# One weight split, the banks of some transposes, the squares of a recurrence and two pads in an encoder layer

## The chip, the cores and the metric

The kernel runs on one core of a Trainium2 chip. The metric is the device time of one execution in microseconds (us). The kernel before has a median of 1216.63 us over three runs, from 1215.02 to 1218.22.

A core has five instruction queues that run side by side and meet only at semaphores: TensorE (PE, matrix products into PSUM; PEld are its weight loads), VectorE (DVE), ScalarE (ACT), GpSimd (POOL) and SyncE (SP, which issues the DMAs here). Within a queue the order is fixed when the program is built. PSUM has eight banks of 128 x 512 fp32 values; TensorE writes them, VectorE and ScalarE empty them.

## The reference

One layer of an encoder over 1024 tokens of width 1024, all in fp32:

```python
h = x + hybrid_mixer(rms_norm(x))          # 8 heads of attention beside a gated linear recurrence
h = h + conv_glu_ffn(rms_norm(h))
return rms_norm(h)

# in hybrid_mixer, for both directions:
a = exp(-8 * sigmoid(xc @ w_a + b_a) * softplus(-lam))
u = sqrt(1 - a * a) * sigmoid(xc @ w_x + b_x) * xc
h_t = a_t * h_(t-1) + u_t                  # forward and reverse; the two are added
y_lru = gelu(lru_g) * h_sum                # then rms_norm over its 512 channels

# conv_glu_ffn:
u = depthwise_conv(xn @ w_up)              # 1024 -> 2 * 2816, three taps along the tokens
return (silu(u[:2816]) * u[2816:]) @ w_down
```

## The kernel before

Every fp32 operand of a product is split into two rounded parts, "hi" and "lo", and three products (hi hi, hi lo, lo hi) are summed. ScalarE mostly writes hi, VectorE or GpSimd lo = source - hi (`split`, lines 59 to 67). A product over 512 contracted values is so 12 matmuls of 128 x 512.

The recurrence works on four channel tiles j = 0 to 3. For each tile TensorE computes the projections into psx and psG and four gates into psg; ScalarE makes tanh, exp and square of them, VectorE and GpSimd scale, scan in two directions and merge into `y_lru`. `squares` (line 239) adds y_lru squared into `qs`: ScalarE squares into a scratch tile, GpSimd adds. The sum is read only at attention step 48. In the loop over j = 0 and 1 the order on TensorE is as written, that of the other engines is set by a scheduler when the program is built; from tile 2 on all are as written.

The FFN's up product uses a seven-product scheme: for each of 22 tiles of hidden channels `prod(1)` to `prod(7)` (line 1060, `PRODUCTS`) multiply sums of token halves (B11, B21, B22, T1 to T4) by sums of weights (W[0] to W[3]). Results lie in eight named PSUM banks: S, T, VL[0], VH[0], VL[1], VH[1], GL, GH.

The seam is the stretch between the output mix and the FFN loop. There the last token tiles are normalised and the eight forms are built: `tr_sum` transposes 128 x 512 values into a spare bank (four instructions of TensorE, line 941), ScalarE and VectorE split them into B[f] ("evict" below). `spare()` hands out banks in turn from the list `spares`. Products of the tiles 0 and 1 are written between the transposes. The weights come by DMA into three staging buffers (pool stp); a fetch is issued when all readers of the buffer's former content are done. The order is as written, but a scheduler may move instructions at the place where the ordered section ends and the next begins (before the FFN loop).

SBUF tiles come from pools on the left and on the right; a right-hand pool grows downward from the top, so a tile that is taken first shifts all tiles of later right-hand pools. Of the operands that TensorE reads T1, T3, T4, cT, wo345, kt1, xch, wn and yl lie on the right; T2, B11, B21, B22, kt0 and all FFN weights lie on the left. In the built program the right-hand ones named begin 32 bytes past a multiple of 64, the left-hand ones on a multiple of 64.

Of the kernel before, what the change touches and what calls it, by code (L numbers as in the profile page):

```python
# [10 lines left out]
F32 = mybir.dt.float32  # L11
# [6 lines left out]
P = 128  # L18
D = 1024
S = 1024  # L20
NT = S // P
# [9 lines left out]
CH = 2  # L31
NCHUNK = NPAIR // CH
EPS = 1e-6
GK = math.sqrt(2.0 / math.pi)

V_CW, V_CB, V_GB, V_LAM, V_GO, V_FW, V_FB = 0, 16, 20, 36, 44, 52, 184
# [4 lines left out]
def encoder_layer(ctx, tc, x, w_in, wq, wk, wv, gw, wo, wup, wdn, vec, g_mix, g_ffn, g_fin, g_q, g_kv, tab_t, tab_n, out):  # L41
    nc = tc.nc
    act, dve, pool, pe = nc.scalar, nc.vector, nc.gpsimd, nc.tensor
# [4 lines left out]
    def sbpool(name, bufs=1, side="left"):  # L48
        return tc.tile_pool(name=name, bufs=bufs, side=side, reuse_waits="tile")
# [10 lines left out]
    def split(hi, lo, src, hi_on="act", lo_on="dve"):  # L60
        if hi_on == "act":
            act.activation(hi, src, AF.Copy)  # L62
        elif hi_on == "dve":
            dve.tensor_copy(hi, src)
        else:
            pool.tensor_scalar(out=hi, in0=src, scalar1=1.0, scalar2=1.0, op0=ALU.mult, op1=ALU.mult)
        (dve if lo_on == "dve" else pool).tensor_tensor(out=lo, in0=src, in1=hi.bitcast(F32), op=ALU.subtract)  # L67
# [68 lines left out]

    right = ExitStack()
    keep = right.enter_context(sbpool("keep", side="right"))
    ctp = ExitStack()
    ctpool = ctp.enter_context(sbpool("ctpool", side="right"))  # L140
    cT = ctpool.tile([P, 2, 3, S], F32R, tag="cT", name="cT")
# [73 lines left out]
    def root():  # L215
        act.activation(bc[:, 0:2, :], bc[:, 0:2, :], AF.Sqrt, scale=-0.0625)
# [22 lines left out]
    def squares(j, t1, eng="act"):  # L239
        if j == 0:  # L240
            act.activation(qs, y_lru[:, j, :], AF.Square)
            return
        if eng == "act":
            act.activation(t1, y_lru[:, j, :], AF.Square)
        else:
            pool.tensor_tensor(out=t1, in0=y_lru[:, j, :], in1=y_lru[:, j, :], op=ALU.mult)
        pool.tensor_tensor(out=qs, in0=qs, in1=t1, op=ALU.add)
# [4 lines left out]
    if True:  # L252
        with sbpool("xp", side="right") as xp:
# [37 lines left out]
                xT.append([xtp.tile([P, NK, 512], F32R, tag="xT", name=f"xT{hf}{z}") for z in range(2)])  # L291
            lat = keep.tile([P, NT, NAT], F32, tag="keepB", name="lat")
            kp_nat = keep.tile([P, S], F32R, tag="kpT", name="kpT")
            ss_x = xp.tile([P, NT], F32, name="ss_x")
            ss_l = xp.tile([P, NT, 2], F32, name="ss_l")

            def square(i):
# [162 lines left out]
        if True:  # L460
            def conv_a(j):
                p = psx[j]
                xc = lp.tile([P, S], F32, tag=f"xc{j % 2}", name=f"xc{j}")
                cw = lambda t: vv[:, V_CW + 4 * j + t:V_CW + 4 * j + t + 1]
                act.activation(xc, p, AF.Identity, scale=cw(2), bias=vv[:, V_CB + j:V_CB + j + 1])
                dve.scalar_tensor_tensor(out=xc[:, 2:], in0=p[:, :-2], scalar=cw(0), in1=xc[:, 2:], op0=ALU.mult, op1=ALU.add)
                dve.scalar_tensor_tensor(out=xc[:, 1:], in0=p[:, :-1], scalar=cw(1), in1=xc[:, 1:], op0=ALU.mult, op1=ALU.add)
                dve.scalar_tensor_tensor(out=xc[:, :-1], in0=p[:, 1:], scalar=cw(3), in1=xc[:, :-1], op0=ALU.mult, op1=ALU.add)
                return xc

            def conv_b(j, xc):
                xch = lp.tile([P, 2, S], F32R, tag="xch", name=f"xch{j}")
                split(xch[:, 0], xch[:, 1], xc, "dve", "dve")
                return xc, xch

            def conv(j):
                return conv_b(j, conv_a(j))

            def gate(j, d, g):
                gwt, xch = got[f"g{j}"], cv[j][1]  # L480
                psg = bigA(f"psg{j}{d}{g}")
                b = 2 * d + g
                for hf in range(2):
                    mm3(psg[:, ts(hf, 512)], (gwt[:, 0, b, :], gwt[:, 1, b, :]),
                        (xch[:, 0, ts(hf, 512)], xch[:, 1, ts(hf, 512)]), True, True)
                act.activation(bc[:, 2 * g + d, :], psg, AF.Tanh, scale=0.5, bias=gb_h[:, 4 * j + b:4 * j + b + 1])

            def gated(j, d):
                dve.scalar_tensor_tensor(out=bc[:, 2 + d, :], in0=bc[:, 2 + d, :], scalar=1.0, in1=cv[j][0], op0=ALU.add, op1=ALU.mult)

            def a_tiles(j):
                return [lp2.tile([P, S], F32, tag="a", bufs=2, name=f"a{j}{d}") for d in range(2)]

            def a2_tile(j, d):
                return lp.tile([P, S], F32, tag="a2", name=f"a2{j}{d}")

            def t1_tile(j):
                return (lp2 if j % 2 else lp).tile([P, S], F32, tag="gt", name=f"t1{j}")

            def load_gates(j, gst=None):  # L500
                if gst is None:
                    gst = stp.tile([P, 4, P], F32, tag="st", name=f"gst{j}")
                    nc.sync.dma_start(out=gst, in_=gw[:, j])
                g = lp.tile([P, 2, 4, P], F32R, tag="gw", name=f"gwt{j}")
                split(g[:, 0], g[:, 1], gst, "act", "pool")
                return g

            got = {"X1": wx1, "G0": wG0, "g0": load_gates(0, gst0)}

            def load(k, j):  # L510
                got[f"{k}{j}"] = load_gates(j) if k == "g" else load_w((0 if k == "X" else 512) + j * P, f"w{k}{j}", w_in, "act")

            cv = {0: conv(0)}
            proj_x(1, got["X1"])
            cv[1] = conv(1)
            order.close()
            order.enter_context(tc.manual_schedule(engines=ORDER_PE))
            for j in range(2):
                load("X", j + 2)
                aa = a_tiles(j)  # L520
                gate(j, 0, 0)
                gate(j, 1, 0)
                for d in range(2):
                    a2 = a2_tile(j, d)
                    decay_exp(j, d, aa[d])
                    square_a(aa[d], a2)
                    decay_tanh(j, d)
                    decay_mul(d, a2)
                proj_g(j, got[f"G{j}"], 0)
                gate(j, 0, 1)  # L530
                gate(j, 1, 1)
                root()
                for d in range(2):
                    gated(j, d)
                    scale_in(d)
                    scan(d, aa[d])
                add_dirs(dve)
                proj_g(j, got[f"G{j}"], 1)
                t1 = t1_tile(j)
                gelu_a(t1, psG[j])  # L540
                gelu_b(t1, psG[j])
                load("g", j + 1)
                load("G", j + 1)
                proj_x(j + 2, got[f"X{j + 2}"])
                if j == 0:
                    cv[2] = conv(2)
                merge(j, t1, dve)
                squares(j, t1)
            load("G", 3)


# [21 lines left out]
    proj_g(2, got["G2"], 1)  # L573
    decay_mul(1, a2)
    root()
    gated(2, 0)
    gated(2, 1)
    scale_in(0)
# [3 lines left out]
    t1 = t1_tile(2)  # L582
# [315 lines left out]
    hh, B, raw = [], {}, {}  # L898
    with sbpool("op", side="right") as op:
# [62 lines left out]
        def tr_sum(f, j, one):  # L962
            src = {"T1": hh[j][:, 0:512], "T2": hh[j + 4][:, 512:1024], "T3": hh[j + 4][:, 0:512], "T4": hh[j][:, 512:1024]}[f]
            to_form(f, j, src, one)
# [54 lines left out]
        W = {(z, 0): wo345[:, z].rearrange("p z (k n) -> p z k n", k=NK) for z in range(1)}  # L1019
# [35 lines left out]
        S1, T1 = bank("S", "s1"), bank("T", "t0")  # L1055
        VL, VH = [None, None], [None, None]
        for j in range(2):
            VL[j], VH[j] = bank(f"L{j}", f"vl{j}"), bank(f"H{j}", f"vh{j}")
        GL, GH = bank("GL", "gl0"), bank("GH", "gh0")
# [10 lines left out]
    def prod(n, j, ps, new):  # L1070
        z, ko, f = PRODUCTS[n]
        w, b = W[z, j], B[f]
        for k in range(4):
            for l, r, a_, z_ in ((0, 0, new and k == 0, False), (0, 1, False, False), (1, 0, False, k == 3)):
                pe.matmul(ps, w[:, l, ko + k, :], b[:, r, k, :], start=a_, stop=z_, skip_group_check=True)  # L1075
# [7 lines left out]
    W[0, 1] = wo345[:, 1].rearrange("p z (k n) -> p z k n", k=NK)  # L1083
    c0 = stp.tile([P, S], F32, tag="st", name="c0")
    tr_sum("T2", 0, spare)
    prod(1, 0, VL[0], True)
    sums_a(7, dve)
    tr_sum("T2", 1, spare)
    tr_sum("T2", 2, spare)
    split(W[0, 1][:, 0], W[0, 1][:, 1], raw[1][0], "act", "dve")  # L1090
    copy(c0[:, lo], VL[0])
    prod(2, 0, GL, True)
    tr2(7, spare)
# [11 lines left out]
    fp = fpx.enter_context(sbpool("fp", side="right"))  # L1105
    for f in ("T1", "T3", "T4"):
        B[f] = fp.tile([P, 2, 4, 512], F32R, name=f)
    C11 = {1: fp.tile([P, S], F32, tag="c", bufs=4, name="s1c")[:, lo]}
    for j in range(3):
        tr_sum("T1", j, spare)  # L1110
    copy(C11[1], S1)
    add(C11[1], VL[1], C11[1])
    prod(6, 0, VL[0], False)
    tr_sum("T1", 3, spare)
    for j in range(3):
        tr_sum("T3", j, spare)
    copy(c0[:, hi], VL[0])
    spares.remove(T1)
    prod(5, 0, T1, True)
    tr_sum("T3", 3, spare)  # L1120
    for j in range(4):
        tr_sum("T4", j, spare)
# [207 lines left out]
    for j in range(1, NPAIR):  # L1330
# [20 lines left out]
        if j == 1:  # L1351
            GH = bank("GH", f"gh{j}")
# [173 lines left out]
```

## Time and profile before

| | us |
|---|---|
| median of three runs (lowest, highest) | 1216.63 (1215.02, 1218.22) |
| the profiled execution, its own time | 1217.72 |
| span of its trace | 1215.9 |
| PE busy in the span | 1165.4 |
| DVE busy | 925.7 |
| ACT busy | 656.4 |
| POOL busy | 241.9 |

The profiled execution takes 1217.72 us, of which the trace spans 1215.9; 1.8 us lie around it. TensorE is busy in 96% of the span, so a look at the whole shows little: what counts are the few places where it waits, and what they wait for. In the page, digits are tenths of busy time in 40 equal slices of 30.4 us. In a timeline, a row gives start, duration, engine, line, operation and, in brackets, how long the engine sat idle before and what ended it. PEclk is the granted clock of TensorE, 1.00 at 2.4 GHz and 0.50 at 1.2 GHz.

### The profile page before, as it was taken

To read this page: it belongs to the slowest core of one execution; us is meant where nothing else is said; L and a number is where in the kernel's file an instruction comes from. 1 tells how busy PE (TensorE), PEld (TensorE's weight loads), DVE (VectorE), ACT (ScalarE), POOL (GpSimd) and SP (SyncE) were. 2 spreads that over 40 slices of the span, in tenths; PEclk is the share of its full clock that TensorE was granted. 3 is DMA by queue.
4 is the path that set the end of the run, shared out by engine and by line. 5 is a ranking of instruction groups with operands and counts; after the bars stand their busy time and mean duration, and the time that the engine had idled before them with its cause. 6 is when DMAs were issued, how large, how long until landed. Compare 5 with 4: busy or idle time off the path is not lost.

```text
span 1215.9 us, 15339 instructions
## 1 busy us (share of the span) xinstructions
PE 1165.4 (96%) x5668; PEld 970.0 (80%) x5668; DVE 925.7 (76%) x1371; ACT 656.4 (54%) x1055; POOL 241.9 (20%) x138
## 2 busy tenths in 40 slices
PE   5999997999999999998999999999999999999997
PEld 5977775788889888776778888888888888888885
DVE  6787879777777755587687877877787876887866
ACT  5736687776777763343554454444454454443453
POOL 2213435621212433352011110101011000000000
PEclk9999989999999999998999999999999999999999
DMA  5311101000000142230243223332323259753233
GB/s 214 98 42 44 44 18 35 18 1 1 1 1 1 53 157 87 73 118 18 61 130 122 96 78 111 106 113 81 110 95 121 87 173 334 262 183 112 96 113 121
DMA packets 93579, 113.38 MB, mean 93 GB/s; under 512 B 5184, under 2 KB 59840, under 8 KB 93504
## 3 DMA queue, kind: packets, MB, share of 16 engines
q1 hardware_dynamic: 93504, 112.40, 27.9%
q8 instruction: 44, 0.72, 0.3%
q14 instruction: 31, 0.25, 0.1%
HBM read 82.76 MB, written 28.57 MB: 92 GB/s over the span
## 4 chain that ended last, share of the span: by engine, by line
PE 82%; DVE 10%; ACT 3%; DMA 2%; issue 2%; SPq 0%; DVEq 0%; POOL 0%; ACTq 0%
PE vl L1075 19%; PE x L1268 9%; PE y L1268 7%; PE gh L1075 5%; PE gl L1075 4%; PE pt L762 4%; PE p L1075 4%; PE av L773 3%; PE av L772 3%; PE sc L70 2%; PE sc L71 2%; PE sc L72 2%; DVE bc L223 2%; PE pso L71 1%; PE pso L72 1%
## 5 line engine op out<-in xcount | busy, mean ns | idle before, releaser
L1075 PE MATMUL vl<-T,w 128*128 128x512 f32 x792 | 195.7, 396 | 1.8 <-ACT gl L1081 1.5
L1075 PEld LDWEIGHTS vl<-T,w 128*128 128x128 f32 x792 | 148.6, 188 | 37.6 <-ACT gl L1081 1.9
L67 POOL TENSOR_TENSOR w<-rg,w 128x1024 fp32r<-128x1024 f32 x21 | 52.0, 2474 | 363.6 <-ACT w L62 212.3
L62 ACT ACTIVATE ptb<-pt 128x512 fp32r<-128x512 f32 x128 | 70.1, 596 | 57.5 <-PE pt L762 56.3
L748 DVE TENSOR_REDUCE nm<-sc 128x1 f32<-128x1024 f32 x64 | 78.2, 1222 | 29.9 <-PE sc L72 29.6
L67 DVE TENSOR_TENSOR ptb<-pt,ptb 128x512 fp32r<-128x512 f32 x128 | 83.1, 681 | 7.0 <-ACT ptb L62 7.0
L755 ACT ACTIVATE pr<-sc,nm 128x1024 f32<-128x1024 f32 x64 | 71.7, 1121 | 4.2 <-DVE nm L748 4.1
L762 PE MATMUL pt<-ident,pr 128*128 128x128 f32 x512 | 67.7, 274 | 3.8 <-DVE ptb L67 3.8
L762 PEld LDWEIGHTS pt<-ident,pr 128*128 128x128 f32 x512 | 59.2, 140 | 14.7 <-DVE ptb L67 6.0
L1075 PE MATMUL gh<-B,w 128*128 128x512 f32 x264 | 64.4, 393 | 1.4 <-DVE T L67 1.4
L1172 ACT ACTIVATE c<-gh,vv 128x512 f32<-128x512 f32 x22 | 17.1, 778 | 89.1 <-DVE gh L1078 89.1
L772 PE MATMUL av<-ptb,vt 128*128 128x256 f32 x256 | 64.9, 292 | 0.0
L773 PE MATMUL av<-ptb,vt 128*128 128x256 f32 x256 | 62.6, 283 | 0.0
L1075 PE MATMUL p<-T,w 128*128 128x512 f32 x252 | 62.5, 397 | 0.0
L1268 PE MATMUL x<-abS 128*128 128x512 f32 x264 | 60.2, 389 | 0.0
L1268 PE MATMUL y<-abS 128*128 128x512 f32 x264 | 60.2, 389 | 0.0
L1075 PEld LDWEIGHTS gh<-B,w 128*128 128x128 f32 x264 | 49.5, 188 | 13.0 <-DVE T L67 1.6
L1075 PE MATMUL vl<-B,w 128*128 128x512 f32 x240 | 58.4, 392 | 0.0
L1268 PEld LDWEIGHTS x<-abS 128*128 128x128 f32 x264 | 49.6, 188 | 10.3
L1268 PEld LDWEIGHTS y<-abS 128*128 128x128 f32 x264 | 49.6, 188 | 10.3
L1075 PE MATMUL gl<-B,w 128*128 128x512 f32 x240 | 57.7, 389 | 0.0
L1075 PEld LDWEIGHTS p<-T,w 128*128 128x128 f32 x252 | 47.4, 188 | 11.4
(646 smaller groups left out, 2953.8 us busy)
## 6 DMA issues: line engine op xcount, KB each, us to landing
rg<-in_wup SPq DMA_DIRECT2D x22, 512.0 KB, 3.9
rv<-in_wup SPq DMA_DIRECT2D x22, 512.0 KB, 3.7
S<-c SPq DMA_DIRECT2D x44, 256.0 KB, 2.6
wr<-in_wdn SPq DMA_DIRECT2D x44, 256.0 KB, 5.4
stS<-S SPq DMA_DIRECT2D x44, 256.0 KB, 2.9
A<-c SPq DMA_DIRECT2D x33, 256.0 KB, 2.1
stA<-A SPq DMA_DIRECT2D x33, 256.0 KB, 4.0
wost<-in_wo SPq DMA_DIRECT2D x8, 512.0 KB, 3.7
```

The lines of the kernel that those rows point to most:

```text
L62: act.activation(hi, src, AF.Copy)
L67: (dve if lo_on == "dve" else pool).tensor_tensor(out=lo, in0=src, in1=hi.bitcast(F32), op=ALU.subtract)
L70: pe.matmul(ps, l[0], r[0], start=start, stop=False)
L71: pe.matmul(ps, l[0], r[1], start=False, stop=False)
L72: pe.matmul(ps, l[1], r[0], start=False, stop=stop)
L748: dve.reduce_max(nm[t], sc[t], axis=AX, negate=True)
L755: act.activation(pr[t], sc[t], AF.Exp, bias=nm[t], accum_out=rowsum[:, h, i:i + 1])
L762: pe.transpose(pt[:, ts(c, P)], pr[t][:, ts(4 * kh + c, P)], ident)
L772: pe.matmul(av[:, 0:256], lv, ptb[buf][:, 0, c, :], start=(c == 0), stop=False)
L773: pe.matmul(av[:, 0:256], lv, ptb[buf][:, 1, c, :], start=False, stop=(c == NT - 1))
L1075: pe.matmul(ps, w[:, l, ko + k, :], b[:, r, k, :], start=a_, stop=z_, skip_group_check=True)
L1268: pe.matmul(ps, ab[:, 0, l, ts(j, P)], ab[:, 1, r, :], start=a_, stop=z_, skip_group_check=True)
```

## The change

Four edits. (1) At the seam the split of W[0, 1] is written ahead of `prod(1, 0)`. (2) The spare banks of the later transposes are listed anew: T1's last and T3's first three may use VH[0], VH[1] and GH; then one takes GH and the T4 forms go to VH[0] and VH[1] by turns. (3) The squares of tiles 0 and 1 are written one tile later. (4) A 32-byte tile (`ss_x`) moves from a later right-hand pool into the first one, and a pad of 24 fp32 (96 bytes) is put beside T1, T3 and T4. In the built program the right-hand tiles named above then begin on a multiple of 64 bytes; qs, y_lru, bc, lat, yn and wo67 stay where they were.

```diff
+PAD = 24
@@
     keep = right.enter_context(sbpool("keep", side="right"))
+    ss_x = keep.tile([P, NT], F32, name="ss_x")
@@
-            ss_x = xp.tile([P, NT], F32, name="ss_x")
@@
                 root()
+                if j == 1:
+                    squares(0, None)
                 for d in range(2):
@@
                 merge(j, t1, dve)
-                squares(j, t1)
@@
     decay_mul(1, a2)
     root()
+    squares(1, t1)
     gated(2, 0)
@@
     tr_sum("T2", 0, spare)
+    split(W[0, 1][:, 0], W[0, 1][:, 1], raw[1][0], "act", "dve")
     prod(1, 0, VL[0], True)
     sums_a(7, dve)
     tr_sum("T2", 1, spare)
     tr_sum("T2", 2, spare)
-    split(W[0, 1][:, 0], W[0, 1][:, 1], raw[1][0], "act", "dve")
@@
         B[f] = fp.tile([P, 2, 4, 512], F32R, name=f)
+    fp.tile([P, PAD], F32, name="pad")
@@
     prod(6, 0, VL[0], False)
+    spares[:] = [VH[0], VH[1], GH]
     tr_sum("T1", 3, spare)
@@
-    spares.remove(T1)
     prod(5, 0, T1, True)
+    spares[:] = [GH, VH[0], VH[1], VH[0], VH[1]]
+    turn[0] = -1
     tr_sum("T3", 3, spare)
```

ScalarE in the recurrence, before: the tanh of tile 1's gelu (L236), the square of y_lru (L244), then the convolution's tap (L465, from psx) and the first two gates (L486, from psg) of the next tiles.

```order
L236 ACTIVATE t_1176<-t_1176 128x1024
L244 ACTIVATE t_1176<-y_lru 128x1024
L465 ACTIVATE xc_1251<-psx_1191,vv 128x1024
L486 ACTIVATE bc<-psg_1259,gb_h 128x1024
L486 ACTIVATE bc<-psg_1267,gb_h 128x1024
```

The same queue with the change, some twelve rows on, where the root (L218) of tile 2 stands; lines count three more by then.

```order
L63 ACTIVATE gwt_1315<-gst_1313 128x512
L218 ACT_TABLE_LOAD
L218 ACTIVATE bc<-bc 128x2048
L246 ACTIVATE t_1176<-y_lru 128x1024
L63 ACTIVATE wkv<-wkvst 128x1024
L234 ACTIVATE t_1369<-psG_1276 128x1024
```

The square of tile 1 stands behind the root; the tap and the gates follow the tanh directly. On GpSimd the add into qs moves from ahead of the gate weights' split to behind it, right ahead of the scaling of the reverse direction (L219). Tile 0's square keeps its place in ScalarE's queue although it is written later.

VectorE at the seam, before (T_4577 is T2, wo_4085 holds W[0, 1], B_4576 is B22, L954 to L960 are the token sums of the last tile).

```order
L67 TENSOR_TENSOR T_4577<-vh_5109,T_4577 128x4x128
L954 TENSOR_TENSOR h_4324<-h_4335,h_4324 128x512
L955 TENSOR_TENSOR h_4335<-h_4335 128x512
L67 TENSOR_TENSOR T_4577<-gh_5111,T_4577 128x4x128
L67 TENSOR_TENSOR T_4577<-t_5105,T_4577 128x4x128
L67 TENSOR_TENSOR wo_4085<-rg_4980,wo_4085 128x1024
L67 TENSOR_TENSOR B_4576<-s_5104,B_4576 128x4x128
```

And with the change:

```order
L68 TENSOR_TENSOR T_4577<-vh_5109,T_4577 128x4x128
L68 TENSOR_TENSOR wo_4085<-rg_4980,wo_4085 128x1024
L957 TENSOR_TENSOR h_4324<-h_4335,h_4324 128x512
L958 TENSOR_TENSOR h_4335<-h_4335 128x512
L68 TENSOR_TENSOR T_4577<-gh_5111,T_4577 128x4x128
L68 TENSOR_TENSOR T_4577<-t_5105,T_4577 128x4x128
L68 TENSOR_TENSOR B_4576<-s_5104,B_4576 128x4x128
```

The split of W[0, 1] moves ahead of four operations; the set of operations up to B22 is the same.

TensorE at the end of the seam, before: from `prod(5)` of tile 0 to `prod(4)` (bank names: t is T, vh_5107 is VH[0], vh_5109 is VH[1], vl_5106 is VL[0]; rows with ident are transposes; T_5209 is T1, T_5210 is T3, T_5211 is T4, B_4576 is B22).

```order
L1075 MATMUL t_5105<-T_5209,w_4911 128x512 x12
L941 MATMUL vh_5109<-ident,h_4335 128x128 x4
L941 MATMUL gh_5111<-ident,h_4318 128x128 x4
L941 MATMUL vh_5107<-ident,h_4320 128x128 x4
L1075 MATMUL vl_5106<-T_5210,w_4977 128x512
L941 MATMUL vh_5109<-ident,h_4322 128x128 x4
L1075 MATMUL vl_5106<-T_5210,w_4977 128x512 x11
L941 MATMUL gh_5111<-ident,h_4324 128x128 x4
L1075 MATMUL gh_5111<-B_4576,w_4840 128x512 x12
L1075 MATMUL vl_5106<-T_5211,w_4911 128x512 x12
```

And with the change:

```order
L1078 MATMUL t_5105<-T_5209,w_4911 128x512 x12
L944 MATMUL gh_5111<-ident,h_4335 128x128 x4
L944 MATMUL vh_5107<-ident,h_4318 128x128 x4
L944 MATMUL vh_5109<-ident,h_4320 128x128 x4
L1078 MATMUL vl_5106<-T_5210,w_4977 128x512 x12
L1078 MATMUL gh_5111<-B_4576,w_4840 128x512 x10
L944 MATMUL vh_5107<-ident,h_4322 128x128 x4
L944 MATMUL vh_5109<-ident,h_4324 128x128 x4
L1078 MATMUL gh_5111<-B_4576,w_4840 128x512 x2
L1078 MATMUL vl_5106<-T_5211,w_4911 128x512 x12
```

GH is free for `prod(3)` early; the last two T4 transposes have moved behind ten matmuls of `prod(3)`. Ahead of `prod(5)` the four transposes go to VH[0], VH[1], GH and VH[0] again, where before they went to VH[1], GH, T and VH[0].

## Rows read from the trace of the kernel before

**Rows 1.** The page's slices of TensorE, tenths busy.

```profile
PE   5999997999999999998999999999999999999997
```

**Rows 2.** Timeline of ScalarE: start, duration, engine, line, operation, idle before.

```profile
152.22 1.06 ACT L244 ACTIVATE t<-y_lru 128x1024 f32<-128x1024 f32 x1 [5.69 <-DVE y_lru L229]
153.19 1.19 ACT L465 ACTIVATE xc<-psx,vv 128x1024 f32<-128x1024 f32 x1
154.28 2.11 ACT L486 ACTIVATE bc<-psg,gb_h 128x1024 f32<-128x1024 f32 x2
...
162.64 1.12 ACT L486 ACTIVATE bc<-psg,gb_h 128x1024 f32<-128x1024 f32 x1 [2.90 <-PE psg L72]
```

**Rows 3.** Timeline of TensorE, recurrence.

```profile
155.43 0.80 PE L70 MATMUL psG<-xT,wG 128*128 128x512 f32 x1 [2.76 <-ACT bc L486]
```

**Rows 4.** Chain of waits: start, length, instruction; recurrence, then seam.

```profile
163.76 0.25 PE psg L72
...
571.39 2.76 PE vl L1075 x12
574.16 0.45 PE vh L941 x4
```

**Rows 5.** Windows: busy of each engine, then PEclk, DMA share, GB/s.

```profile
155.00:158.00 3.00, 2.57 (x6) 2.09 (x7) 2.93 (x3) 2.97 (x4) 0.71 (x1) 0.50 0.00 0
...
575.00:578.00 3.00, 1.70 (x12) 1.34 (x11) 2.49 (x4) 2.19 (x5) 0.00 (x0) 1.00 0.00 0
```

**Rows 6.** Timeline of GpSimd and of VectorE, tile 2 of the recurrence.

```profile
172.74 3.25 POOL L219 TENSOR_TENSOR bc<-bc 128x1024 f32<-128x1024 f32 x1 [2.37 <-ACT wkv L62]
175.95 4.39 POOL L67 TENSOR_TENSOR wkv<-wkvst,wkv 128x1024 fp32r<-128x1024 f32 x1
...
173.77 4.38 DVE L223 TENSOR_TENSOR_SCAN bc<-a,bc 128x1024 f32<-128x1024 f32 x1
...
179.18 3.32 DVE L223 TENSOR_TENSOR_SCAN bc<-a,bc 128x1024 f32<-128x1024 f32 x1
```

**Rows 7.** Timeline of all engines, seam and first tiles of the FFN.

```profile
557.60 0.68 DVE L954 TENSOR_TENSOR h<-h,h 128x512 f32<-128x512 f32 x1
...
560.12 1.22 DVE L67 TENSOR_TENSOR wo<-rg,wo 128x1024 fp32r<-128x1024 f32 x1
...
561.40 4.64 PE L1075 MATMUL vl<-B,wo 128*128 128x512 f32 x10 [2.58 <-DVE wo L67]
...
562.58 0.69 DVE L960 TENSOR_TENSOR h<-h,h 128x512 f32<-128x512 f32 x1
...
577.20 3.06 PE L1075 MATMUL t<-T,w 128*128 128x512 f32 x12 [1.30 <-DVE T L67]
...
587.26 3.02 PE L1075 MATMUL gh<-B,w 128*128 128x512 f32 x12 [1.41 <-DVE T L67]
...
589.20 0.38 SPq L1138 DMA_DIRECT2D rg<-in_wup  x1
...
593.66 1.06 ACT L62 ACTIVATE w<-rg 128x1024 fp32r<-128x1024 f32 x1 [1.10 <-DMA rg<-in_wup]
...
598.97 3.07 PE L1075 MATMUL vl<-T,w 128*128 128x512 f32 x12 [0.31 <-ACT gh L1081]
...
614.69 3.04 PE L1075 MATMUL vl<-T,w 128*128 128x512 f32 x12 [1.51 <-ACT gl L1081]
```

**Rows 8.** The page's groups: busy us, mean ns of one, idle before.

```profile
L67 DVE TENSOR_TENSOR ptb<-pt,ptb 128x512 fp32r<-128x512 f32 x128 | 83.1, 681 | 7.0 <-ACT ptb L62 7.0
...
L62 ACT ACTIVATE ptb<-pt 128x512 fp32r<-128x512 f32 x128 | 70.1, 596 | 57.5 <-PE pt L762 56.3
...
L1075 PE MATMUL p<-T,w 128*128 128x512 f32 x252 | 62.5, 397 | 0.0
...
L1075 PE MATMUL vl<-B,w 128*128 128x512 f32 x240 | 58.4, 392 | 0.0
L1075 PE MATMUL gl<-B,w 128*128 128x512 f32 x240 | 57.7, 389 | 0.0
```

## The prediction

> **What bounds the kernel now.** I read the page's slices first. TensorE stands at 9 in every slice but the first, the seventh (the end of the recurrence) and the nineteenth (the seam) [rows 1]. So an edit is worth what it takes from a wait of TensorE, or from the chain that TensorE waits for, and the time then stays gained, since TensorE is full from there on. Next I read, in the timelines, the waits of TensorE that each edit touches.
>
> In the recurrence ScalarE squares tile 1 only when VectorE has merged it, after 5.69 us idle, and the tap and the first gates of the next tiles stand behind it in the queue [rows 2]. The psG product waits 2.76 us for the first of these gates to leave its bank [rows 3], and TensorE then falls to 1.2 GHz [rows 5]. The chain goes on from TensorE's last gate matmul at 163.76 [rows 4].
>
> At the seam there are three waits of TensorE: 2.58 us for the split of W[0, 1], 1.30 us for bank T, 1.41 us for bank GH [rows 7].
>
> **Squares of the recurrence.** Without the square ahead of it the tap no longer waits for the merge. TensorE's two gates, 12 matmuls of 0.23 us (12 take 2.76 [rows 4]), end where it starts to wait, at 152.7 (155.43 less 2.76), so they begin at 149.9, and psx, ahead of them in the queue, is complete by then. The tap takes its 1.19 us from about 150, the first gate follows at about 151.4 and frees its bank by 152.4, before TensorE comes to psG. The 2.76 us go. From 155.43 to 164.01 TensorE ran 24 matmuls of psG and gates in 8.58 us [rows 3, 4]; at the full clock they take 24 x 0.23 = 5.5 us, so they end at 158.2. ScalarE is the later one: its work from 154.28 to its idle time at 159.74 is 5.46 us [rows 2]; started at 151.4, and with the second gate ready at 152.7, it ends at 157.3. The third gate then runs at 157.3 instead of 162.64: 5.3 us earlier, and ScalarE and VectorE stand in an unbroken chain behind it.
>
> The square (1.06 us) now lies behind the root on ScalarE, beside VectorE work; what follows it there is not late. Its add on GpSimd is not free. [Rows 6] show how the two engines take turns: GpSimd's scaling ends at 175.99, the first scan, though begun at 173.77, ends at 178.15, 2.16 us after it; GpSimd's split of wkv, begun at 175.95, ends at 180.34, 2.19 us after the scan; the second scan ends at 182.50, 2.16 us after that. Each took about 2.2 us once the other had ended. The add is one more turn of 2.2 us, ahead of the scaling, for which the second scan waits as data. With the shift of 5.3 the turn that was the scaling's (from 173.8) begins at 168.5 and goes to the add, until 170.7; first scan until 172.9, scaling until 175.1, then wkv's split, which needs no signal, until 177.3, second scan until 179.5. So 5.3 - 2.2 = 3.1 us are gained. If the scan gets ahead of wkv's split, it is 5.3; if another turn slips in, 1.0. Tile 0's square stays where it was in its queue, so the like wait there stays.
>
> The Trainium skill ("SBUF — State Buffer", section "Who interferes with whom") says that a VectorE instruction with two SBUF inputs and a GpSimd instruction that reads SBUF exclude each other for a whole instruction. By that rule the add costs its full turn and the gain is 3.1; if the two merely shared a port it would be nearer 5. The trace agrees with the rule (4.38 against 2.2 us).
>
> **The split at the seam.** VectorE's list up to the token sums is the same, so the sums' end, 563.27, does not move [rows 7]. The split itself moves from 560.12 to the slot at 557.60 and ends at 558.82, so the product's third matmul starts at 558.9 instead of 561.40. Ten matmuls take 2.3 us, to 561.2, and then TensorE waits for the sums until 563.3, since the next transposes read them. So a wait of 2.6 us becomes one of 0.3 and one of 2.1. From 563.3: four transposes 0.45, twelve matmuls 2.76, twelve transposes 1.35 [rows 4], so prod(6) starts at 567.9 instead of 571.39: 3.5 us at the full clock. Before, ten matmuls ran in 4.64 us, half the clock, after the wait.
>
> **The banks.** Ahead of prod(5) bank T is free, but the fourth transposes go to the bank of the first, whose eviction they await: 0.45 + 0.60 + 0.68 [rows 8] and some 0.1 of signals is 1.8, another 0.45 makes 2.3 us from the end of prod(6). Before it was 577.20 - 574.15 = 3.05. Gain 0.75.
>
> After prod(5) the wait for GH goes, but something else comes. T4's last two transposes now stand behind 11 + 10 matmuls: counted from prod(5)'s end (580.26 before) T3's last part is evicted at 1.84, 21 matmuls of 0.23 run to 6.7, eight transposes to 7.6, ScalarE evicts until 8.2, VectorE until 8.95. Only then does VectorE add VH[0] (0.69) and split the first weights of tile 1 (1.22), until 10.9. That split is the last reader of a staging buffer, and SP issues the next fetch at its end: before at 589.20, that is 8.94 [rows 7]. So the fetch is 2.0 us later. ScalarE's split waits in order for it (593.66, 1.10 us after its last work), and 5.3 us on ScalarE copies the bank for which TensorE waits 0.31 us at 598.97. TensorE itself comes there a little sooner than before, as prod(4) has to wait for the add's read of VL[0] until 9.65 and three products follow to 17.9, while ScalarE is ready at 20.7. The wait of 0.31 grows to about 2.8 us. Net of the seam at the full clock: -3.5 - 0.75 + 2.0 = -2.2.
>
> Two waits of 2.1 and 2.8 us remain or arise. The clock fell after those of 2.58 and 2.76 us and stood at 1.00 beside the one of 1.30 [rows 5]. One fall costs between 0 and 3.1 (the 8.58 against 5.5 us), nearest 2.3 (the ten matmuls). I take one fall, 2.3. So the seam comes to 0: the same idle time in other places. Its ends are -2.2 and +3.5.
>
> **The pads.** T1's product (p) has 397 ns a matmul, B11's (vl<-B) 392, B21's (gl<-B) 389 [rows 8], with the same shapes, the same engine always full; T1, T3 and T4 lie 32 bytes past a multiple of 64, the B forms on one. If the place is the cause, 5 ns on 20 tiles x 36 matmuls is 3.6 us; the first two tiles lie under waits. The bounds are 0 (it is something else) and 8 ns, 5.8 us. I take 3.6, since the like-for-like partner is 392. The other moved tiles (scores of odd heads, the mix) add some tenths either way.
>
> The Trainium skill (same page, "Specifications (TRN2)") gives SBUF lines of 16 bytes as the grain. By that rule a start on a multiple of 32 is as good as one of 64 and the pads change nothing. No row shows a moved tile, so the rule stands as the first rival.
>
> **Sum.** -3.1 + 0 - 3.6 = -6.7 against the profiled execution's 1217.72 (span 1215.9 and 1.8 around it): 1211.0. The median lies 1.1 lower, inside the runs' spread of 3.2, and gives 1209.9. I forecast 1210.5, midway; the rivals stand on the same footing.
>
> **Rivals.**
> - The pads do nothing: 1210.5 + 3.6 = 1214.1. For it: no moved tile has been seen. Against: the three products on shifted forms and those on the others differ though all else is alike.
> - The seam keeps the full clock in both waits: -2.2 instead of 0, 1208.3; with the second scan ahead of wkv's split 1206.1. For it: the 2.1 us is nearer to none than 2.58.
> - The squares' gain is eaten, because GpSimd's extra turn or another wait of VectorE holds the chain: 1213.6. Against: the count of turns above leaves nothing over for a further one, and each engine's order is fixed.
> - Slower: the late fetch does not heal. In the FFN loop TensorE waits for ScalarE's copy, which stands behind a split that waits for a fetch. If each of the 20 tiles after the seam keeps 1.51 us of it, as tile 2 has now [rows 7], that is +30: 1241. It decides from 0.52 us a tile (6.7 + 3.7 over 20). Against: before, tile 2 has that wait and no later tile, so the loop has slack to recover.
>
> **Chances.** The forecast 0.60, pads nothing 0.15, seam better 0.13, squares eaten 0.08, slower 0.04. A measurement of this kernel tells about 0.3% (3.65 us) from no change, so faster means below 1213.0: nearly all of the first and third case, a third of the second and of the fourth: 0.80. Same 0.15, slower 0.05. The likeliest case's own range is 1208 to 1213; the range for 8 in 10 reaches 1206 to 1214.5.
>
> **What would show it.** The psG product of tile 2 follows the gates without idle time, at PEclk 1.00; the second scan of tile 2 ends about 3 us earlier. TensorE waits about 2 us for the token sums ahead of T2's last transposes, and 2 to 3 us for ScalarE's copy ahead of prod(7) of tile 1. The p group falls to about 392 ns. It is wrong if p stays at 397, if TensorE waits for ScalarE's copies in many FFN tiles, or if the recurrence ends no earlier.

## The result and the profile after

| | before | after |
|---|---|---|
| median, us (lowest, highest) | 1217.43 (1215.02, 1219.09) | 1204.74 (1203.41, 1205.71) |
| profiled execution, us | 1217.72 | 1204.22 |
| span, us | 1215.9 | 1202.4 |
| PE busy, us | 1165.4 | 1154.3 |

The ratio is 0.9891, with a 95% interval from 0.9873 to 0.991: 12.7 us faster. The forecast was 1210.5, with a range from 1206.0 to 1214.5. The sign was right, the size too small; the time fell 1.3 us below the range.

To find the 12.7 us I take each instruction of TensorE in both traces, in the order of the program, and subtract its start in before from its start in after. This shift changes only where a stretch takes another time. A seam is called unchanged below in before and in every run without the seam's edit.

| run | 0-150 us | 150-300 (recurrence) | 300-545 (attention, mix) | 545-618 (seam) | 618-1000 (FFN loop) | whole |
|---|---|---|---|---|---|---|
| after | -1.66 | -3.61 | +1.37 | -1.74 | -7.87 | -13.50 |
| after, second run | +1.16 | -3.55 | +0.16 | -2.75 | -7.87 | -12.86 |
| pad alone | +0.74 | +0.07 | +0.11 | -1.49 | -7.87 | -8.42 |
| squares alone | +2.03 | -3.41 | +1.92 | -1.21 | 0.00 | -0.68 |
| seam alone | +0.98 | +0.11 | +1.80 | -1.29 | 0.00 | +1.60 |
| ss_x alone | +0.26 | -0.06 | +1.36 | -2.38 | 0.00 | -0.82 |

(Shift gained in each stretch of before's time axis, us. Minus is earlier.) The loop and the recurrence repeat to 0.2 us and follow their edits. The other stretches vary by up to 3.7 us between runs that do the same there.

The loop's rows, in the loop alone (640 to 980 us), TensorE, line of the products: count, then shortest/median/longest duration in ns. Of before:

```profile
L1075 PE MATMUL vl<-B,w x211: 387/393/398, 648.1 to 980.0; 128*128 128x512 f32 x106
L1075 PE MATMUL p<-T,w x204: 392/396/403, 650.9 to 964.5; 128*128 128x512 f32 x102
L1075 PE MATMUL gl<-B,w x204: 388/389/390, 656.4 to 970.0; 128*128 128x512 f32 x102
```

The same of after:

```profile
L1078 PE MATMUL vl<-B,w x216: 389/389/389, 641.9 to 968.0; 128*128 128x512 f32 x108
L1078 PE MATMUL p<-T,w x216: 389/389/389, 644.6 to 970.7; 128*128 128x512 f32 x108
L1078 PE MATMUL gl<-B,w x216: 389/389/389, 650.0 to 976.2; 128*128 128x512 f32 x108
```

Every matmul now takes 389 ns, and the spread is gone. The vl<-B row, which [rows 8] gave as 392 and which the prediction took for undisturbed, fell as well, and p fell to 389 and not to the 392 of the forecast. Matmuls overlap, so the cost is read from the starts. Timeline of TensorE in before, three products of 12 (T4, B11, T1):

```profile
604.63 2.98 PE L1075 MATMUL vl<-T,w 128*128 128x512 f32 x12
607.45 2.92 PE L1075 MATMUL vl<-B,w 128*128 128x512 f32 x12
610.21 2.04 PE L1075 MATMUL p<-T,w 128*128 128x512 f32 x8
```

and in after:

```profile
599.08 2.88 PE L1078 MATMUL vl<-T,w 128*128 128x512 f32 x12
601.80 2.88 PE L1078 MATMUL vl<-B,w 128*128 128x512 f32 x12
604.52 2.88 PE L1078 MATMUL p<-T,w 128*128 128x512 f32 x12
```

From start to start, T4's product took 2.82 us and takes 2.72; B11's took 2.76 and takes 2.72. So 0.10 us goes from each of the three T products and 0.04 from each of the three that follow one (T2, B11, B22). That is 0.4 us a tile and about 8 us in 20 tiles; the shift says 7.87.

The recurrence went as forecast. ScalarE in after [rows 2]:

```profile
148.30 1.21 ACT L466 ACTIVATE xc<-psx,vv 128x1024 f32<-128x1024 f32 x1 [3.38 <-PE psx L73]
149.74 1.12 ACT L487 ACTIVATE bc<-psg,gb_h 128x1024 f32<-128x1024 f32 x1 [0.23 <-PE psg L73]
...
155.50 1.10 ACT L487 ACTIVATE bc<-psg,gb_h 128x1024 f32<-128x1024 f32 x1
```

The tap waits for psx and no longer for the merge, and the first gate is done before TensorE comes to psG at 150.91, which has no wait now [rows 3]. The third gate runs at 155.50 instead of 162.64, 5.5 us earlier beside the 1.65 that TensorE was ahead already. Then come the turns, GpSimd first and VectorE below, in after [rows 6]:

```profile
165.58 3.27 POOL L249 TENSOR_TENSOR qs<-qs,t 128x1024 f32<-128x1024 f32 x1 [2.36 <-ACT t L246]
168.81 4.38 POOL L221 TENSOR_TENSOR bc<-bc 128x1024 f32<-128x1024 f32 x1
173.16 2.40 POOL L68 TENSOR_TENSOR wkv<-wkvst,wkv 128x1024 fp32r<-128x1024 f32 x1
```

```profile
166.61 4.39 DVE L225 TENSOR_TENSOR_SCAN bc<-a,bc 128x1024 f32<-128x1024 f32 x1
...
173.23 4.49 DVE L225 TENSOR_TENSOR_SCAN bc<-a,bc 128x1024 f32<-128x1024 f32 x1 [1.11 <-POOL bc L221]
```

The ends are 168.85 (add), 171.00 (scan), 173.19 (scaling), 175.56 (wkv's split), 177.72 (second scan): turns of 2.15 to 2.4 us, in the order forecast. The second scan ended at 182.50 before; less the 1.65, it is 3.1 us earlier, the number of the prediction.

The seam, TensorE in after [rows 7] (L962 are the token sums, vh L1081 is an add on VectorE, gh L1084 a copy on ScalarE):

```profile
554.17 3.38 PE L1078 MATMUL vl<-B,wo 128*128 128x512 f32 x12
558.67 0.66 PE L944 MATMUL vh<-ident,h 128*128 128x128 f32 x4 [1.13 <-DVE h L962]
...
568.46 3.00 PE L1078 MATMUL t<-T,w 128*128 128x512 f32 x12
...
581.43 5.75 PE L1078 MATMUL vl<-T,w 128*128 128x512 f32 x24 [1.72 <-DVE vh L1081]
...
591.90 4.52 PE L1078 MATMUL vl<-T,w 128*128 128x512 f32 x12 [2.00 <-ACT gh L1084]
```

The wait for the split is gone. One of 1.13 us for the token sums took its place (forecast 2.1), prod(4) waits 1.72 us for the add, and prod(7) of tile 1 waits 2.00 us for ScalarE's copy (forecast 2.8). Behind that wait the clock fell. Windows of after, with PEclk in the third column from the end:

```profile
592.00:595.00 3.00, 3.00 (x10) 2.35 (x11) 1.15 (x1) 0.36 (x1) 0.00 (x0) 0.68 0.23 87
595.00:598.00 3.00, 3.00 (x12) 2.44 (x11) 1.44 (x3) 0.15 (x1) 0.00 (x0) 0.75 0.00 0
```

### The profile page after: what moved, and what is told of

Same layout as the page of the kernel before. It is cut to its first block, busy times and chain, and to the rows that moved or that the text cites. A ratio compares the mean times of both kernels' runs of the same rounds, so it can differ in the third digit from the quotient of the medians.

```text
span 1202.4 us, 15336 instructions
## 1 busy us (share of the span) xinstructions
PE 1154.3 (96%) x5668; PEld 966.8 (80%) x5668; DVE 925.8 (77%) x1371; ACT 655.9 (55%) x1055; POOL 242.7 (20%) x138
## 4 chain that ended last, share of the span: by engine, by line
PE 75%; DVE 7%; ACT 1%; issue 1%; DMA 1%; DVEq 0%; POOL 0%; ACTq 0%
PE vl L1078 19%; PE x L1274 10%; PE y L1274 7%; PE gh L1078 5%; PE gl L1078 5%; PE pt L765 4%; PE p L1078 4%; PE av L776 3%; PE av L775 3%; PE sc L71 2%; PE sc L73 2%; PE sc L72 2%; PE pso L73 1%; PE pso L72 1%; PE pso L71 1%
## 5 line engine op out<-in xcount | busy, mean ns | idle before, releaser
L1078 PE MATMUL vl<-T,w 128*128 128x512 f32 x792 | 192.5, 392 | 5.6 <-ACT gh L1084 2.0
```

## The experiments

**One edit at a time.** Four kernels: before with one edit each.

The pad (pad_only), the squares (squares_only), the seam (seam_only) and ss_x (keep_only):

```diff
+    fp.tile([P, 24], F32, name="pad")
```

```diff
+                if j == 1:
+                    squares(0, None)
@@
-                squares(j, t1)
@@
+    squares(1, t1)
```

```diff
+    split(W[0, 1][:, 0], W[0, 1][:, 1], raw[1][0], "act", "dve")
     prod(1, 0, VL[0], True)
@@
-    split(W[0, 1][:, 0], W[0, 1][:, 1], raw[1][0], "act", "dve")
@@
+    spares[:] = [VH[0], VH[1], GH]
@@
-    spares.remove(T1)
@@
+    spares[:] = [GH, VH[0], VH[1], VH[0], VH[1]]
+    turn[0] = -1
```

```diff
+    ss_x = keep.tile([P, NT], F32, name="ss_x")
@@
-            ss_x = xp.tile([P, NT], F32, name="ss_x")
```

> The kernel before with the pad beside T1, T3 and T4 alone; nothing else moves. Theory A (a form that starts 32 bytes past a multiple of 64 slows its own product and the first matmuls of the product behind it): all seven products of the FFN loop start a matmul every 226.7 ns, the loop is 7.9 us shorter, and the time is about 1209.5 where the kernel before has 1217.4. Theory B (the working of the prediction: 5 ns for the matmuls of the three shifted products alone): the loop is 3.6 us shorter, about 1213.8, and the rest of the 7.9 us came from the seam or the weights' timing. Theory C (the place does nothing): 1217.4. Ahead of the FFN loop all three expect a shift of less than 0.5 us.

Measured: 1208.81, ratio 0.9939 (0.9916 to 0.9961). The loop is 7.87 us shorter, as in after. Its rows:

```profile
L1075 PE MATMUL vl<-B,w x216: 389/389/389, 646.9 to 973.1; 128*128 128x512 f32 x108
L1075 PE MATMUL p<-T,w x216: 389/389/389, 649.7 to 975.8; 128*128 128x512 f32 x108
```

So the pad alone makes the whole gain of the loop. Theory A's size is right, and theory B, the working of the prediction, falls. In the built program T1, T3 and T4 begin at 96 within 128 bytes in before and at 0 in this kernel and in after; the B forms, T2 and the FFN weights begin at 0 in all three.

> The kernel before with the squares of the recurrence moved, and nothing else. Theory A (the working of the prediction: 2.76 us of waiting for psG and the half clock go, 2.2 us come back as GpSimd's extra turn): TensorE is 3.1 to 3.4 us ahead from attention to the end, about 1214.2 where the kernel before has 1217.4. Theory B (part of the 3.3 us came from the shifted right-hand tiles): under 2 us, above 1215.4. Neither moves the seam or the FFN loop by more than 0.5 us against each other.

Measured: 1215.08, ratio 0.9984 (0.9967 to 1.0002). The time alone doesn't settle it; the shift does: -3.41 us from 150 to 300 us, against +0.11 to -0.06 in the kernels without the edit, and nothing in the loop. So theory A holds.

> The kernel before with the split of W[0, 1] ahead of the product and the new lists of spare banks, and nothing else. Theory A (the seam alone): TensorE is about 1.7 us ahead at 620 us and stays so through the FFN loop, about 1215.7 where the kernel before has 1217.4. Theory B (the changed timing of the weights at the seam also gave the loop part of its 7.9 us): 1.7 us at 620 us and 4 to 6 us at 1000 us, about 1212. Theory C (the working of the prediction: one fall of the clock eats what the waits give): 0 +- 0.5 us.

Measured: 1219.18, ratio 1.0004 (0.9985 to 1.0023). The seam gains 1.29 us against before's profile and the loop nothing, so theory B falls. But the kernels whose seam is unchanged gain as much there: 1.49 (pad alone), 1.21 (squares alone), 2.38 (ss_x alone). Before's own profile had an unusually dear seam. The next rows are TensorE behind the same 2.58 us wait, for which before took 4.64 us [rows 7]. With the pad alone:

```profile
562.33 3.92 PE L1075 MATMUL vl<-B,wo 128*128 128x512 f32 x10 [2.58 <-DVE wo L67]
```

and with the squares alone:

```profile
561.90 3.43 PE L1077 MATMUL vl<-B,wo 128*128 128x512 f32 x10 [2.58 <-DVE wo L67]
```

and with ss_x alone, where the granted clock stays at 1.00 through the whole seam:

```profile
562.96 2.60 PE L1075 MATMUL vl<-B,wo 128*128 128x512 f32 x10 [2.58 <-DVE wo L67]
```

The same instructions behind the same wait took 4.64, 3.92, 3.43 and 2.60 us: whether the clock falls to 1.2 GHz, when, and for how long differs from run to run. Over all thirteen profiles the seam with the edit gains 1.29 to 2.75 us against before's profile (mean 1.7, eight profiles), without it 0 to 2.92 (mean 1.6, five, before's own included). The edit is worth 0.1 us, which can't be told from nothing.

Three of these profiles show the granted clock at 1.00 all through the seam, so the edit can be judged without a fall: ss_x alone gains 2.38 us and w_shift (below) 2.92, both with the seam of before, and the second run of after, with the edit, 2.75. Counted from 545 us, the profiles with the edit are 4.0 to 4.1 us ahead of before at 574 us, and 5.3 at 580 us; of that 2.8 are before's own fall of the clock, since ss_x alone and w_shift are 2.8 ahead there too. By 600 us the waits for the add and for ScalarE's copy have taken back all but 2.5 to 3.2. So the edit moves the idle time and does not shorten it: theory C's time is right, though one fall of the clock is not what makes it so.

> The kernel before with the 32-byte tile ss_x in the first right-hand pool, and nothing else: the other right-hand tiles, but not T1, T3 and T4, begin on a multiple of 64. Theory A (the place of a moving operand counts): the scores of odd heads start a matmul every 231.6 instead of 233.2 ns, some 0.4 us over the attention, about 1217.0 where the kernel before has 1217.4. Theory B (the 1.6 us that TensorE is ahead at 20 us also come from the place): 2.0 us, 1215.4. If those 1.6 us are the chance of which engine gets its turn first, they are not in this run or are there without a pattern.

Measured: 1216.81, ratio 0.9996 (0.9979 to 1.0013). The attention gains 0.20 us (300 to 495 us), half of what theory A expected: the scores of odd heads start every 231 instead of 233 ns. The start gains nothing, so theory B falls. The 1.5 us that after had gained by 22 us are no work of ss_x.

**What "the right place" is.** Three kernels that put the T forms or the weights elsewhere.

pad8 and t1_shift are after with the first and the second edit; w_shift is before with the third.

```diff
-PAD = 24
+PAD = 8
```

```diff
-PAD = 24
+PAD = 8
@@
         B[f] = fp.tile([P, 2, 4, 512], F32R, name=f)
+        if f == "T1":
+            fp.tile([P, 8], F32, name="pad0")
```

```diff
     fw = ctx.enter_context(sbpool("fw"))
+    fw.tile([P, 24], F32, name="wpad")
```

> The changed kernel with a pad of 32 instead of 96 bytes: T1, T3 and T4 begin on a multiple of 64 that is no multiple of 128, all else as in the changed kernel. Theory A (the moving operand must start on a multiple of 64): all seven products of the FFN loop stay at 226.7 ns a matmul, about 1204.7. Theory R (the moving operand and the weights must lie alike within 128 bytes; the weights lie at 0): T1, T3 and T4 run at 231 to 235 ns and the products behind them are slowed in their first matmuls, the loop is 4 to 8 us longer than in the changed kernel, about 1210 to 1212.

Measured: 1211.93, ratio 0.9953 (0.9939 to 0.9968). The loop gains 2.36 us instead of 7.87. Its rows:

```profile
L1078 PE MATMUL vl<-B,w x216: 387/393/398, 646.8 to 977.8; 128*128 128x512 f32 x108
L1078 PE MATMUL p<-T,w x213: 388/394/398, 649.6 to 979.8; 128*128 128x512 f32 x107
L1078 PE MATMUL gl<-B,w x204: 389/389/389, 655.1 to 966.7; 128*128 128x512 f32 x102
```

A multiple of 64 that is none of 128 is not good enough. So the "multiple of 64" of the prediction was wrong, and theory A falls.

> The kernel before, with its T forms at 96 within 128 bytes, and the FFN weights of half of the slots shifted by 96 bytes, so that in about half of the products the weights lie at 96 too and in the others at 0. Theory R (moving operand and weights must lie alike within 128 bytes): T products with shifted weights run at 226.7 to 230 ns a matmul, and B and T2 products with shifted weights at 233 to 235; the loop is some 1 us longer than before. Theory A (the start of the moving operand counts, wherever the weights are): the intervals are those of the kernel before, 234.6 for T1, T3 and T4 and 229.8 behind them, and the time is unchanged (1217).

Measured: 1216.96, ratio 0.9992 (0.9975 to 1.0009). The time says nothing, since products won and lost; the rows of single products do. T4's product at 721 us has weights at 96 like T4 itself, the one at 740 us has weights at 0, B21's at 732 us has weights at 96 and B21 at 0:

```profile
L1075 PE MATMUL vl<-T,w x11: 389/389/395, 721.4 to 723.7; 128*128 128x512 f32 x11
```

```profile
L1075 PE MATMUL vl<-T,w x11: 392/396/402, 740.8 to 743.2; 128*128 128x512 f32 x11
```

```profile
L1075 PE MATMUL gl<-B,w x11: 392/397/400, 732.5 to 734.9; 128*128 128x512 f32 x11
```

T4 has not moved, yet runs at 389 where the weights lie as it does; B21, which ran at 389 in before, runs at 397 where they do not. So the moving operand and the weights must lie alike within 128 bytes, as theory R says. The loop as a whole came out 0.2 us shorter than in before, where some 1 us longer was expected.

It is not all that counts. T3's product at 677 us has T3 and its weights at 96, and B21's ahead of it has B21 and its weights at 0, so neither is mismatched, and B21's ends at 227 ns a matmul:

```profile
L1075 PE MATMUL gl<-B,w x11: 389/389/398, 674.2 to 676.5; 128*128 128x512 f32 x11
```

```profile
L1075 PE MATMUL vl<-T,w x11: 387/393/397, 677.0 to 679.3; 128*128 128x512 f32 x11
```

Yet the first nine matmuls of T3's product start 224 to 236 ns apart (232 on average), and only the last three 227. The down product of this kernel shows the same: its two operands always lie alike, in some products both at 0, in the others both at 96. A product right behind such a switch averages 230 to 231 ns a matmul, all others 226.7, and the stretch from 1000 to 1205 us, with some 30 switches, takes 1.25 us longer than in before. So a change of place from one product to the next costs about as much as following a mismatched product does.

> The changed kernel with T1 alone 32 bytes past a multiple of 64 (T3 and T4 on one). Carry-over theory: prod(5) on T1 runs at 234.6 ns a matmul, the first eight matmuls of prod(6) on T2, which follows it, at about 231.5, and all other products at 226.7; the loop is 20 x (12 x 7.9 + 8 x 4.6 ns) = 2.6 us longer than in the changed kernel. Rival (each product is slowed by its own operand alone, and T2 and B were slow for another reason): prod(6) at 226.7 too, 1.9 us longer.

Measured: 1211.86, ratio 0.9953 (0.9935 to 0.9971). The loop gains 1.85 us against before, 6.0 less than after. T3 and T4 lay at 64 within 128 here, which the expectation took for a good place; they ran at 230.3 ns from start to start, T1 (at 32) at 233.6, and T2, B11 and B22 behind them at 229.7 to 230.8. So it repeats pad8 for T3 and T4 and does not test the carry-over alone. The next run does.

```diff
         B[f] = fp.tile([P, 2, 4, 512], F32R, name=f)
+        if f == "T1":
+            fp.tile([P, 24], F32, name="pad0")
```

> The changed kernel with T1 alone at 32 within 128 bytes, T3 and T4 at 0 like the weights. Carry-over theory: prod(5) on T1 at 233.6 ns a matmul and prod(6) behind it at 229.9 (its first eight matmuls slow), all other products at 226.7; the loop is 20 x 12 x (6.9 + 3.2 ns) = 2.4 us longer than in the changed kernel. Rival (a product is slowed by its own operands alone): prod(6) at 226.7, 1.7 us longer.

Measured: 1208.11, ratio 0.993 (0.991 to 0.995). The loop is 1.90 us longer than in after. Its rows:

```profile
L1078 PE MATMUL vl<-T,w x636: 389/389/395, 642.4 to 978.5; 128*128 128x512 f32 x159
L1078 PE MATMUL vl<-B,w x216: 389/389/389, 645.1 to 973.0; 128*128 128x512 f32 x108
L1078 PE MATMUL p<-T,w x216: 392/396/400, 647.8 to 975.8; 128*128 128x512 f32 x108
```

The p product is slow throughout. Of T2's, which follows it, only the first three matmuls start 231 to 232 ns apart, the other nine 227. There is a carry-over, but over three matmuls and not the eight expected, and the 1.90 us lie nearer the rival's 1.7 than the 2.4 of the carry-over theory. With 96 bytes it was eight matmuls, with 64 ten. The offset alone does not set this: in t1_shift T1 lay at 32 too, behind a product that was slow itself, and T2's first seven matmuls were slow. Why it lasts as long as it does stays open.

**A kernel that beats both.** First every operand of TensorE, but for eight small matmuls that read qs, on a multiple of 128, by placing three small tiles anew:

```diff
-    ss_x = keep.tile([P, NT], F32, name="ss_x")
@@
             kp_nat = keep.tile([P, S], F32R, tag="kpT", name="kpT")
-            ss_l = xp.tile([P, NT, 2], F32, name="ss_l")
+            ss_x = ss_h = keep.tile([P, NT], F32, tag="ssx", name="ss_x")
+            ss_l = keep.tile([P, NT, 2], F32, tag="ssl", name="ss_l")
@@
-        ss_h = op.tile([P, NT], F32, tag="ssh", name="ss_h")
```

> The changed kernel with the small sums ss_x, ss_l and ss_h put on top of the first right-hand pool, so that every operand of TensorE begins on a multiple of 128: also scores, mix, queries, gates and the latent product. Theory R: scores, mix, gates and queries come down from 230 to 233 ns to 226.7 a matmul; over 384 + 336 + 96 + 96 + 48 + 42 matmuls at 4 to 6.5 ns some 5 us, less where TensorE waits: 3 to 5 us under the changed kernel, about 1200.5. Theory A (a multiple of 64 is enough, and those products are slow for another reason): 1204.7, no difference from the changed kernel.

Measured: 1204.56, ratio 0.9891 (0.9872 to 0.9911), the same as after. The mix came down from a median of 394 to 389 ns and the gates from about 230 to 227 ns from start to start. In after both operands of the gates lay at 64, alike, but the psG and psx products around them at 0, so this is the switch once more. The scores came down only from 231.6 to 230.9, and those of even heads, at 0 all along, ran at 231.5 too, so the scores have another cause, which stays open. The attention gained 1.0 us against after (300 to 495 us), and no more than that is seen. The expected 3 to 5 us were too many.

Then tile 0's square, which in after stands where it stood before:

```diff
-                if j == 1:
-                    squares(0, None)
@@
+    squares(0, None)
     squares(1, t1)
```

> The kernel with every operand of TensorE on a multiple of 128, in which tile 0's square is also written later, beside tile 1's, so that it leaves ScalarE's queue where it stood ahead of the tap and the gates of tile 2. If the wait of 4.4 us ahead of psG at 122 us goes as that at 155 us went: TensorE is 2.5 to 4 us ahead from there; 1 to 2 us of it come back beside the later squares, where ScalarE has 1.06 us more. Against the changed kernel some 2 us, and about 1 us from the places: about 1201.5. Rival (the chain on VectorE and ScalarE through the merge and the taps of the next tile sets the end, not the square): the wait stays and the time is that of the changed kernel, 1204.6.

Measured: 1199.31 (1197.31 to 1201.71), ratio 0.9867 (0.9841 to 0.9892). After, timed beside it, had 1205.43. The wait of TensorE in after:

```profile
121.79 0.61 PE L71 MATMUL psG<-xT,wG 128*128 128x512 f32 x1 [4.36 <-ACT bc L487]
```

and in this kernel:

```profile
117.08 0.50 PE L71 MATMUL psG<-xT,wG 128*128 128x512 f32 x1 [0.53 <-ACT bc L487]
```

3.8 us of waiting went, and of the half clock behind it (122 to 130 us) 1.6 us against after and 2.4 against the kernel before this edit. That is 5.4 us and more where 2.5 to 4 were expected, and the rival falls. The second square beside the first cost nothing in the recurrence's end (-3.58 us from 150 to 300 us, as without it).

**The changed kernel once more.**

> The changed kernel once more, timed beside the two others. Theory (turns of VectorE and GpSimd and falls of the clock come out differently from run to run): the stretches that no edit touches (0 to 22, 122 to 150, 495 to 545 us) differ from the first profile by one or two steps of 0.7 to 1.7 us, while recurrence, FFN loop and down product repeat within 0.2 us; about 1204.7.

Measured: 1205.43 (1204.31 to 1209.27), ratio 0.9917 (0.9893 to 0.994). Recurrence and loop repeat (-3.55, -7.87). By 22 us it is 0.8 us behind before's profile, where the first run was 1.5 ahead; in the mix it loses 0.35 instead of 1.6 us. At the start these are turns that fall out differently; for the mix that is not shown. VectorE's scaling of the second token tile in before, beside a GpSimd split:

```profile
15.05 2.85 DVE L312 SCALAR_TENSOR_TENSOR xall<-xall,rx1r,g 128x1024 f32<-128x1024 f32 x1
```

and the same in the first run of after:

```profile
15.36 1.28 DVE L313 SCALAR_TENSOR_TENSOR xall<-xall,rx1r,g 128x1024 f32<-128x1024 f32 x1
```

and in its second run, the same program:

```profile
15.38 2.85 DVE L313 SCALAR_TENSOR_TENSOR xall<-xall,rx1r,g 128x1024 f32<-128x1024 f32 x1
```

So the program does not decide it, and ss_x alone did not bring the short form either (2.85). The medians of before in the three groups of runs were 1217.31, 1217.82 and 1216.29, with single runs from 1211.33 to 1221.41.

## Why the prediction was too small

- **Pads: the term that was mis-sized.** The prediction put it at 3.6 us: 5 ns (397 less 392) on the T products alone, "since the like-for-like partner is 392", with 5.8 us as the upper bound. It measured 7.9 us, outside these bounds: by the starts some 5.7 on the T products (8 ns a matmul) and 2.3 on the products behind them. The partner, vl<-B, stands right behind T4's product and was slowed by it; the clean row was gl<-B with 389. Each T product lost 0.10 us and each product behind one 0.04, and the second were not counted at all. With 7.9 in the sum the forecast would have been 1206.2, inside the stated range, above the runs of after (1203.41 to 1205.71) and among those of its repeat (1204.31 to 1209.27).
- **Its reason was half right.** The place was the cause, as forecast. But not "a multiple of 64": moving operand and weights must lie alike within 128 bytes, and like those of the products beside them. That the pad of 96 bytes fits both was luck.
- **The first rival fell.** The Trainium skill ("SBUF — State Buffer", section "Specifications (TRN2)") gives lines of 16 bytes; by that grain pads of 32 and of 96 bytes would be alike and neither would do anything. Their loops differ by 5.5 us.
- **Squares: right.** 3.1 forecast; 3.4 to 3.6 measured on TensorE, 3.1 on the second scan, with the order of turns as worked out. The Trainium skill (same page, section "Who interferes with whom") has the two engines exclude each other for a whole instruction; the trace agrees: the scan that met the add ended 2.15 us behind it, and not beside it.
- **Seam: right for the edit, by other sizes.** Forecast 0 (-2.2 to +3.5). Both waits came at their places, 1.13 instead of 2.1 and 2.00 instead of 2.8 us, and one fall of the clock. Against before's profile it is -1.7, against all profiles of the unchanged seam -0.1. Part of this is luck: 2.8 of what the split seemed to give (3.5 forecast, 4.0 measured at 574 us) was the fall of the clock in before's own profile, which two other profiles of the unchanged seam do not have.
- **The lasting late fetch (the rival on the other side): no.** The loop lost nothing behind 620 us.
- **What is left.** -3.5 - 0.1 - 7.9 - 0.2 (scores) is -11.7; the medians say -12.7 (-11.0 to -15.5 by the interval). The rest is within what turns and clock falls change from run to run.

## What to carry to other kernels

Compare a matmul's duration with its shortest form in the whole trace, not with a neighbour: a product behind a slow one is slow too. Place the operands of a full TensorE loop so that the starts of all of them agree within 128 bytes, from product to product too; it costs a pad and gave 0.65% here. And before a wait is judged by one profile, look at it in a second: the same seam took between 0 and 2.9 us less in runs that did the same.

## What the runs showed of the hardware

- In the FFN loop and the down product a 128x512 fp32r matmul starts every 226.7 ns where the starts of moving operand and weights agree within 128 bytes (0 and 0, or 96 and 96) and those of the product before lay there too. It starts every 230.3 ns with the moving operand at 64 and the weights at 0, 233.6 to 233.8 ns at 32 and 0, 234.6 ns at 96 and 0, and the next product's first three to ten matmuls are slowed too. Going from 0 and 0 to 96 and 96, or back, slows the first eight or nine (230 to 231 ns over the product).
- The same wait need not cost the clock. TensorE waits 1.70 us for ptb at 228 to 230 us in before, and the granted clock stays at 1.00. In the run with the pad alone it waits 1.76 us, and these windows follow, 1.5 us dearer:

```profile
230.00:233.00 3.00, 3.00 (x19) 2.82 (x18) 2.56 (x4) 2.29 (x4) 0.45 (x1) 0.63 0.00 0
233.00:236.00 3.00, 3.00 (x17) 2.68 (x17) 0.61 (x2) 0.38 (x1) 0.00 (x0) 0.80 0.00 0
```
